# Rotary embedding of split heads: the first run of 1024 rows loaded and stored as two and six rows per partition

## The chip, the cores and the metric

One core of a Trainium2 chip runs the kernel. The metric is device time in microseconds (us) of one execution; the kernel before has a median of 161.52 us over three runs (161.49 to 161.65). The engines of the core work at the same time, each on its own list of instructions: PE (TensorE, matrix products), DVE (VectorE), ACT (ScalarE), POOL (GpSimd) and SP (SyncE, here only stores). They meet through semaphores. Data move between the large memory (HBM) and the on-chip memory of 128 partitions by 16 DMA engines, fed by two queues here: the loads that ACT issues and the stores that SP issues.

## The reference

The input `x` has 16 batches of 512 positions with 1024 values (16 heads of 64), `cos` and `sin` have one row of 32 values for each position. Each head is rotated:

```
x1, x2 = x[..., :32], x[..., 32:]          # in each head
out = concat(x1*cos - x2*sin, x1*sin + x2*cos)
```

All is float32: 33.6 MB are read and 33.6 MB written.

## The kernel before

**Rows, runs, tiles.** Two batches make a run of 1024 positions. A partition holds 8 neighbouring positions of it, so that a run is 8 "rows" of 128 partitions by 1024 values, and the whole is 8 runs or 64 rows, counted by `u`. The list `tiles` (lines 41 to 46) says in which pieces a run is loaded and stored: (run, first row, number of rows). Runs 1 to 6 go in one piece of 8 rows (4 MB, in each partition one stretch of 32 KB); runs 0 and 7 in two pieces of 4 rows (2 MB, 16 KB stretches). There are 10 loads and 10 stores. `x_sb` is a ring of 40 rows, in which a row is computed in place: five runs fit.

**What a row costs in instructions.** DVE multiplies the row by the cosines into PSUM (line 286, `mul`). POOL multiplies the row with its halves swapped by the signed sines into `t2_sb` (line 252), for two neighbouring rows in one instruction where `joined` says so; rows 0 to 3 and the last two are single. Row 3 of a run that is one piece is done by DVE instead (line 279; `V2`, `V_ROW`). The sum of the two products is made by DVE (line 297, `comb`) or, for rows with `PE2` (rows 1, 3 and 5 of a run, from row 4 on and up to row 59), by PE, which adds the second product through an identity matrix (line 216), and ACT, which moves the result back into `x_sb` (line 183). DVE's order is `mul(u)`, then `comb(u - 1)`. Before the first row of a tile (`r == 0`) both POOL and DVE wait for that tile's load, on `sem_in[t]`.

**The start.** ACT issues load 0, then the two loads of the tables `cos` and `sin`, then the other loads that fit the ring (lines 165 to 173). It makes `pick` from an identity matrix (line 176); PE waits for `pick` and both tables and spreads the tables over the partitions (line 200); ACT copies the sines to `s_sb` (lines 178 and 179). Only then can POOL and DVE start.

**Loads later on, and stores.** The loads of runs 5 to 7 need places of the ring that runs 0 to 2 give up. ACT issues them between its own instructions, after rows 17, 25 and 33, and waits first for all stores of run 0, 1 or 2 (lines 184 to 187; `stores_of` counts the stores of a run). SP goes through the rows, and at the last row of each tile it waits until all sums up to that row are made (`wait_added`) and issues the tile's store (lines 154 to 160).

Of the kernel before, what the change touches and what calls it, by code (L numbers as in the profile page):

```python
# [6 lines left out]
def bass_split_heads_rope_kernel(  # L7
# [21 lines left out]
    R1 = seq // P  # L29
    R2 = 2 * R1  # L30
# [10 lines left out]
    tiles = []  # L41
    for c in range(runs):
        if c in (0, runs - 1):
            tiles += [(c, 0, R1), (c, R1, R1)]
        else:
            tiles.append((c, 0, R2))
    NT = len(tiles)
# [300 lines left out]
```

## Time and profile before

| | us |
|---|---|
| median of three runs | 161.52 (161.49 to 161.65) |
| the profiled execution | 161.35 |
| its span, first to last instruction | 159.9 |
| POOL busy, of this line 252 | 131.8, 131.1 |
| DVE busy, of this lines 286, 297, 279 | 129.3, 76.7, 52.3, 7.3 |
| PE busy, ACT busy | 66.7, 23.7 |
| moved | 67.25 MB, 420 GB/s over the span |

The profile is one execution taken by the hardware profiler. Its page gives busy time for each engine and the span in 40 slices of 4 us, with the busy tenths of each engine and of the DMA engines. A share of the DMA engines a little over 1 comes from transfers that overlap on one engine. Other views of the same trace give instructions in order of time, the chain of work that ended last, busy time in chosen windows, and for a line that issues transfers the time from issue to landing. "Landing" is when the semaphore of a transfer has its full count.

### The profile page before, as it was taken

What the parts mean: (1) busy time and instruction counts of PE and PEld (TensorE: products, weight loads), DVE (VectorE), ACT (ScalarE), POOL (GpSimd) and SP (SyncE); (2) the same over time, 40 slices, a digit from 0 to 9 for tenths busy, and PEclk for the clock granted to TensorE, in tenths of its full rate; (3) what the DMA queues carried; (4) which work ended last, traced back from release to release, by engine and by line L of the source; (5) the groups of instructions that cost most, each with busy time, mean ns of one, the idle gap of its engine ahead of it and who ended that gap; (6) DMA issues with size and microseconds to landing.
All of it is one profiled execution on the core that took longest, in us unless ns stands there. A gap on an engine that the chain in (4) does not pass through costs nothing.

```text
span 159.9 us, 494 instructions
## 1 busy us (share of the span) xinstructions
PE 66.7 (42%) x94; PEld 22.6 (14%) x94; DVE 129.3 (81%) x115; ACT 23.7 (15%) x25; POOL 131.8 (82%) x41
## 2 busy tenths in 40 slices
PE   6050006338932762286209540098509860880000
PEld 1020002012301220122002110022102220220000
DVE  0009986799999999999799927999999989989700
ACT  0410000202220222020400204002500250031000
POOL 1009999999999999999999999599999999598000
PEclk9999999999995799569965998555985589567555
DMA  5999998999999999999999999999999999999896
GB/s 164 411 441 459 393 508 344 447 406 426 471 406 447 479 393 395 492 418 402 418 492 393 418 492 402 402 475 389 479 397 418 451 418 488 410 402 484 373 438 279
DMA packets 3169, 67.25 MB, mean 420 GB/s; under 512 B 352, under 2 KB 608, under 8 KB 608
## 3 DMA queue, kind: packets, MB, share of 16 engines
q10 hardware_dynamic: 1728, 33.69, 49.8%
q1 hardware_dynamic: 1440, 33.56, 48.7%
q14 instruction: 1, 0.01, 0.0%
HBM read 33.69 MB, written 33.55 MB: 420 GB/s over the span
## 4 chain that ended last, share of the span: by engine, by line
DMA 49%; DVE 16%; POOL 13%; issue 7%; PE 6%; ACT 2%; ACTq 1%; DVEq 0%; SPq 0%
DMA x_sb<-in_x_dram 27%; DMA out_dram<-x_sb 18%; POOL t_sb L252 13%; DVE x_sb L297 8%; DVE t_ps L286 6%; PE t_ps L216 5%; DMA stage<-in_sin_dram 4%; DVE t_sb L279 2%; ACT x_sb L183 1%; PE tab_ps L200 1%; ACTq L152 0%; ACTq L173 0%; ACT s_sb L178 0%; ACT s_sb L179 0%; DVE tab_ps L265 0%
## 5 line engine op out<-in xcount | busy, mean ns | idle before, releaser
L252 POOL TENSOR_TENSOR t_sb<-x_sb,s_sb 128x2048 f32<-128x2048 f32 (+1 forms) x35 | 131.1, 3775 | 14.9 <-ACT s_sb L179 10.3
L216 PE MATMUL t_ps<-t_sb,ident 128*128 128x512 f32 x84 | 61.9, 888 | 70.6 <-DVE t_ps L286 48.8
L286 DVE TENSOR_TENSOR t_ps<-x_sb,tab_ps 128x1024 f32<-128x1024 f32 x64 | 76.7, 1221 | 17.4 <-ACT s_sb L179 10.5
L297 DVE TENSOR_TENSOR x_sb<-t_ps,t_sb 128x1024 f32<-128x1024 f32 x43 | 52.3, 1219 | 3.2 <-POOL t_sb L252 3.1
L183 ACT ACTIVATE x_sb<-t_ps 128x1024 f32<-128x1024 f32 x21 | 21.3, 1024 | 111.6 <-PE t_ps L216 100.2
L216 PEld LDWEIGHTS t_ps<-t_sb,ident 128*128 128x128 f32 x84 | 20.7, 273 | 111.4 <-DVE t_ps L286 78.8
L279 DVE TENSOR_TENSOR t_sb<-x_sb,tab_ps 128x1024 f32<-128x1024 f32 x6 | 7.3, 1215 | 0.0
L200 PE MATMUL tab_ps<-stage,pick 128*128 128x256 f32 x4 | 2.0, 667 | 4.8 <-DMA stage<-in_sin_dram 4.8
L193 PE MATMUL t_ps<-zero 128*128 128x512 bf16 x6 | 2.7, 630 | 1.3 <-DVE zero L260 1.3
L200 PEld LDWEIGHTS tab_ps<-stage,pick 128*128 128x128 f32 x4 | 1.2, 324 | 5.9 <-issue 5.7
L176 ACT ACT_TABLE_LOAD x1 | 1.3, 1283 | 4.8 <-issue 4.8
L193 PEld LDWEIGHTS t_ps<-zero 128*128 128x128 bf16 x6 | 0.7, 138 | 2.3 <-DVE zero L260 1.2
L178 ACT ACTIVATE s_sb<-tab_ps 128x256 f32<-128x256 f32 x1 | 0.4, 384 | 4.4 <-PE tab_ps L200 4.4
L260 DVE MEMSET zero<- 128x256 uint32 x1 | 0.3, 272 | 0.9 <-PEq L330 0.9
L227 POOL MEMSET ident<- 128x128 f32 x1 | 0.2, 205 | 0.3 <-POOLq L330 0.3
L176 ACT ACTIVATE pick<-ident 128x256 f32<-128x256 f32 x1 | 0.4, 430 | 0.0
L179 ACT ACTIVATE s_sb<-tab_ps 128x256 f32<-128x256 f32 x1 | 0.4, 378 | 0.0
L229 POOL TENSOR_SCALAR_AFFINE_SELECT ident<-ident 128x128 f32<-128x128 f32 x1 | 0.3, 294 | 0.1
L330 POOL MEMSET const-float32-0.0<- 128x1 f32 x1 | 0.1, 99 | 0.3 <-issue 0.3
L265 DVE TENSOR_SCALAR tab_ps<-tab_ps 128x32 f32<-128x32 f32 x1 | 0.2, 189 | 0.0
L330 POOL MEMSET const-bfloat16-1.0<- 128x1 bf16 x1 | 0.1, 102 | 0.0
L330 POOL MEMSET const-uint8-127<- 128x1 uint8 x1 | 0.1, 102 | 0.0
(1 smaller groups left out, 0.1 us busy)
## 6 DMA issues: line engine op xcount, KB each, us to landing
x_sb<-in_x_dram ACTq DMA_DIRECT2D x6, 4096.0 KB, 33.5
out_dram<-x_sb SPq DMA_DIRECT2D x6, 4096.0 KB, 25.0
x_sb<-in_x_dram ACTq DMA_DIRECT2D x4, 2048.0 KB, 19.9
out_dram<-x_sb SPq DMA_DIRECT2D x4, 2048.0 KB, 14.9
stage<-in_cos_dram ACTq DMA_DIRECT2D x1, 64.0 KB, 7.3
stage<-in_sin_dram ACTq DMA_DIRECT2D x1, 64.0 KB, 7.0
```

The lines of the kernel that those rows point to most:

```text
L176: ae.activation(pick[:], ident[:].rearrange("q (s h) -> q h s", h=2)[:, :, None, :].broadcast_to([P, 2, 2, P // 2]), COPY).then_inc(sem_g, 1)
L178: ae.activation(s_sb[:, :, 0, :].rearrange("p (h r) d -> p h r d", h=2), tab_ps[:, :, 1], COPY, scale=-1.0)
L179: ae.activation(s_sb[:, :, 1, :].rearrange("p (h r) d -> p h r d", h=2), tab_ps[:, :, 1], COPY).then_inc(sem_s, 1)
L183: ae.activation(xs[:, u % RING, :], t1_ps[:, u % NT1, :], COPY).then_inc(sem_a, 1)
L193: pe.matmul(t1_ps[:, k, b * BANK:(b + 1) * BANK], zero[:, 0:P], zero[:], start=True, stop=True).then_inc(sem_w, 1)
L200: pe.matmul(tab_ps[:, h].rearrange("p c r d -> p (c r d)"), pick[:, h].rearrange("q b s -> q (b s)"), stage[:].rearrange("q c f -> q (c f) ...
L216: ins = pe.matmul(t1_ps[:, u % NT1, b * BANK:(b + 1) * BANK], ident[:], t2[:, b * BANK:(b + 1) * BANK], start=False, stop=True, skip_group ...
L252: pl.tensor_tensor(t2_sb[:, u % NT2:u % NT2 + n], x_sb[:, k:k + n, :, ::-1, :], table[:, :, None, :, :].broadcast_to([P, n, H, 2, HALF]), ...
L279: ve.tensor_tensor(t2_sb[:, u % NT2, :, :, :], swapped(k), over_heads(tab_ps[:, 0, 1, V_ROW - 1:V_ROW + 1, :]), mult)
L286: ve.tensor_tensor(t1_ps[:, u % NT1, :].rearrange("p (h d) -> p h d", d=HALF), x_sb[:, k, :, :, :].rearrange("p h t d -> p (h t) d"), tab_ ...
L297: ve.tensor_tensor(xs[:, k, :], t1_ps[:, u % NT1, :], t2_sb[:, u % NT2, :, :, :].rearrange("p h t d -> p (h t d)"), add,).then_inc(sem_v, 1)
L330: nc = _bacc.Bacc("TRN2", target_bir_lowering=False, num_devices=1)
```

## The change

Run 0 is cut after its second row in place of its fourth. Run 7 stays as it is.

```
     for c in range(runs):
         if c in (0, runs - 1):
-            tiles += [(c, 0, R1), (c, R1, R1)]
+            n = R1 // 2 if c == 0 else R1
+            tiles += [(c, 0, n), (c, n, R2 - n)]
         else:
             tiles.append((c, 0, R2))
```

Load 0 and store 0 become 1 MB (8 KB in a partition), load 1 and store 1 become 3 MB (24 KB). The waits for loads are then ahead of rows 0 and 2 in place of 0 and 4, and SP issues the first two stores after rows 1 and 7 in place of 3 and 7. `PE2` and `joined` go by row numbers and stay the same, as does `V2`, since neither piece of run 0 has eight rows. The number of instructions does not change.

More of the change, by code (lines that the diff above doesn't have):

```diff
@@ L43, in bass_split_heads_rope_kernel @@
         if c in (0, runs - 1):
-            tiles += [(c, 0, R1), (c, R1, R1)]
+            n = R1 // 2 if c == 0 else R1
+            tiles += [(c, 0, n), (c, n, R2 - n)]
         else:
```

## The prediction

> **What bounds the kernel now.** I read the page's slices first.
>
> ```profile
> span 159.9 us, 494 instructions
> ...
> PE 66.7 (42%) x94; PEld 22.6 (14%) x94; DVE 129.3 (81%) x115; ACT 23.7 (15%) x25; POOL 131.8 (82%) x41
> ...
> DMA  5999998999999999999999999999999999999896
> GB/s 164 411 441 459 393 508 344 447 406 426 471 406 447 479 393 395 492 418 402 418 492 393 418 492 402 402 475 389 479 397 418 451 418 488 410 402 484 373 438 279
> ```
>
> POOL and DVE look like bounds at some 82%, but the DMA engines are full in every slice except the first and the last ones. The busy time by windows says it sharper (us of the window; then each engine's busy time; last: clock, DMA share, GB/s):
>
> ```profile
> 0.00:2.00 2.00, 0.75 (x2) 0.28 (x3) 0.27 (x1) 0.00 (x0) 0.70 (x6) 1.00 0.39 74
> 2.00:4.00 2.00, 2.00 (x5) 0.46 (x3) 0.00 (x0) 0.00 (x0) 0.00 (x0) 1.00 0.78 254
> ...
> 30.00:40.00 10.00, 4.49 (x5) 1.67 (x6) 10.00 (x10) 1.39 (x2) 10.00 (x3) 1.00 1.01 428
> ...
> 120.00:130.00 10.00, 8.93 (x11) 3.24 (x12) 9.59 (x10) 2.05 (x2) 9.92 (x3) 0.54 0.98 419
> ```
>
> The reader is to see shares of 0.98 to 1.01 from 30 to 130 us: transfers that are ready wait for engines, whatever computes. Third, the chain of waits, for the two places where computing and transfers touch, the start and the end:
>
> ```profile
> 1.68 7.03 DMA stage<-in_sin_dram
> 8.71 0.14 issue
> 8.85 2.06 PE tab_ps L200 x4
> ...
> 11.67 9.48 POOL t_sb L252 x5
> ...
> 95.53 42.55 DMA x_sb<-in_x_dram
> 138.09 0.07 issue
> 138.16 6.85 POOL t_sb L252 x2
> ...
> 148.41 2.35 DVE x_sb L297 x2
> ```
>
> Computing starts at 11.67 because the sine table lands at 8.71, behind load 0 in ACT's queue (load 0: issued 0.80, 7.5 to landing, 8.3). It ends with the last load, landed at 138.09: the last store is issued at 150.83. Fourth, the landings of single transfers (a store's line, its time to landing):
>
> ```profile
> L160 SPq DMA_DIRECT2D out_dram<-x_sb x1: 376/376/376, 22.3 to 22.3; - x1
> ...
> DMA to landing us min/median/max: 19.3/19.3/19.3
> ...
> L160 SPq DMA_DIRECT2D out_dram<-x_sb x1: 332/332/332, 150.8 to 150.8; - x1
> ...
> DMA to landing us min/median/max: 9.1/9.1/9.1
> ```
>
> Store 0 lands at 41.6; by the same rows store 1 (issued 33.67, 22.6) at 56.3, the next at 75.6 and 95.1, the last three at 150.2, 155.1 and 159.9. Loads: 8.3, 13.56, 23.3, 36.9, 51.4, 70.4, 89.6, 109.0, 123.6, 138.1.
>
> **What a partition's run costs.** 128 partitions over 16 DMA engines are 8 runs on each. Load 2 (32 KB runs) takes 23.3 - 13.56 = 9.74, so 1.218 us a run; load 1 (16 KB) 13.56 - 8.71 = 4.85, 0.606 a run. Store 1 against loads of 32 KB takes 56.3 - 41.6 = 14.7 = 8 x (0.606 + 1.218 = 1.824) = 14.6; the 4 MB stores 19.3 to 19.5 = 8 x 2.436. So the two queues take turns run by run, whatever the size of a run. All runs together: 64 x 0.606 + 96 x 1.218 = 155.7, the tables 0.4 (8.71 - 8.3), and 8.3 - 4.85 = 3.45 before load 0 is at full rate: 159.5, against a span of 159.9. Only some 0.4 us is not pure transfer.
>
> The change makes runs of 8 and 24 KB, which the trace does not show. In proportion they cost 0.303 and 0.912; a run of 32 KB costs twice one of 16 KB, so no fixed part is seen. The upper bound is a whole table run (512 B, 16 of them in 0.41, 0.026) added to each of 16 runs, 0.4 us in all; the lower bound is that the shortfall of the second window (254 of 430 GB/s for 2 us, 0.8 us) halves with the smaller first runs, -0.4. I take 0, since the 16 and 32 KB rows are the nearest.
>
> **The change, part by part.** Instructions, waits and the order on each queue stay the same: ten loads, ten stores. Only two loads and two stores change size, and store 0 is due after row 1 in place of row 3.
>
> Start. Load 0 loses 8 x 0.303 = 2.43 us; the tables would land at 6.28. PE also needs ACT's `pick`, done at 6.52 (6.09 + 0.43, behind the table load at 4.79). So PE starts at 6.6 in place of 8.85: **2.25 us earlier**, POOL at 9.4. Bounds: 0 to 2.3. The page "DMA: Bandwidth & Descriptors" of the Trainium skill, section "Measured", gives 6.15 us for 1 MB and asks for pieces of at least 1 MiB; by its fit in "Anatomy of one DMA" (2.0 us fixed and bytes by 436 GB/s) an estimate for 1 MiB is 4.4 us. By the fit the tables would land at 5.6 and `pick` would still decide; by the line for 1 MB at 7.4 (0.8 + 6.15 + 0.4), and 1.3 us would be left of 2.25.
>
> Rows 2 and 3 now wait for load 1, whose bytes end where they did, at 13.56. POOL wants row 2 at 9.4 + 2 x 2.31 = 14.04, and is not held. DVE wants it at 15.26 - 2.25 = 13.01, is held 0.6, and makes it good in its idle 2.11 before 25.51. Behind its wait stand the rest of its own instructions, and row 1's addition: store 0 goes out at 16.0 (22.30 before). Store 1 goes out at 33.67 - 2.25 = 31.4.
>
> The store queue. Store 0 landed 19.3 after its issue, 14.7 of that in transfer: 4.6 us pass before an idle store queue gets its turns beside 32 KB loads. Now: store 0 from 20.6, 8 x (0.303 + 1.218) = 12.2, to 32.8; store 1 from 31.4 + 4.6 = 36.0, 8 x (0.912 + 1.218) = 17.0, to 53.0. Before it was 56.3. The next store (49.99 - 2.25 = 47.7, + 4.6 = 52.3) is there in time. So the **stores run 3.3 us ahead** from here on, and as the engines are full, every run that a store takes earlier a load takes later: the loads land 3.3 us later. Bounds: 1.0 if computing starts no earlier (55.3), and 4.0 where the next store's own start, 52.3, decides (a store 1 that follows store 0 with no gap).
>
> The middle. Loads 3.3 later: row 40's at 92.9. POOL wanted it at 93.0 (row 8 at 29.84, and four times three pairs of 4.49 and a single of 2.31), now at 90.8. DVE has by then gained more than 2.25, since its 4.14 us behind ACT's wait for the store of run 2 (95.1, now 91.8) moves with that store. POOL so waits about as long as computing is ahead (2.1 of 2.25), and row 48's load, at 112.3, is in the same relation: no net price here.
>
> The end. The last load lands at 138.1 + 3.3 = 141.4. Behind it: POOL's pair 4.51, then six DVE instructions (five starts 1.13 apart and 1.22: 6.9) and the issue, 0.15: the last store goes out at 153.0 in place of 150.83. Is that late? The store before it lands at 155.1 whatever happens, and 4.8 later the last one is through. An idle queue takes 7.5 for these 2 MB (load 0, a cold start); 4.85 of transfer and 1.4 to 1.9 of latency, an estimate from 4.6 less two 32 KB runs, make 6.5. So the end is 153.0 + 6.5 to 7.5 = 159.5 to 160.5, or the engines' own 159.9 where that is later: **+0 to +0.6**, and I take +0.2. The cover is the backlog in SP's queue, worth 9.1 - 6.5 to 7.5 = 1.6 to 2.6 us; the issue comes 2.2 later.
>
> Sum: start -2.25, hidden by full engines; loads +3.3, hidden by the backlog but for 0.2; span 160.1. The profiled execution took 161.35 us, 1.45 around the span, and the median is 161.52, 0.17 more: 160.1 + 1.45 + 0.15 = **161.7 us**.
>
> **Rivals.** A measurement of this kernel can tell some 0.2% (0.32 us) from no change.
>
> (a) Slower: the last store finds idle engines. One mechanism, stores ahead and loads behind; it decides once the loads are over 3.3 us late. At the upper bound of 4.0 and 7.5 for the store: 138.1 + 4.0 + 11.6 + 7.5 = 161.2, +1.3: **162.8 us**. If the store queue has no gap at all and the next store follows at 49.8, 6.5 late: 163.7 and 165.3 us. For it: the cover is thin by my own count, 1.6 to 2.6 against 2.2. Against: the engines are full, so a later load leaves no byte undone, only the last 2 MB badly placed. Chance 0.40.
>
> (b) Faster by the start: 2.25 reach the end, 161.52 - 2.25 = **159.3 us**. For: POOL has hardly a gap from 11.67 to 99.7. Against: the shares near 1.0, and the floor of 159.5 for the span. The page "Perfetto Trace Analysis" of the Trainium skill, "DMA Optimizations", says smaller pieces may help if the DMA engines are generally idle; here they are not, so by that rule nothing is gained either. Chance 0.04.
>
> (c) Faster within the floor: the 0.4 us over 159.5 go, and 0.4 of the start's shortfall: **160.7 us**. For: sixteen engines need not end as unevenly as now. Against: nothing in the change evens them. Chance 0.10.
>
> (d) The start does not move (tables or `pick` late): store 1 at 55.3, loads 1.0 later, inside the cover: **161.5 us**, counted with no change.
>
> **How the numbers follow.** Forecast with (d): 0.46; (a) 0.40; (b) and (c) 0.14. So faster 0.14, same 0.46, slower 0.40. The likeliest one's own range is 161.2 to 161.9. The range for all takes in (c) and most of (a): 160.8 to 163.6.
>
> **What would show it.** POOL's first product at 9.4; store 0 issued at 16.0 and store 1 at 31.4; store 1 landed near 53; the last load landed near 141.4; the last store issued near 153.0 and landed 6.5 to 7.5 later. Wrong would be: the last load no later than before (the turns are not by run), DMA shares below 0.95 in the middle (engines run dry), or a gap over 2 us in the DMA ahead of the last store.

## The result and the profile after

The changed kernel takes 1.0049 times the time before (95% interval 1.003 to 1.0069), +0.8 us with +0.5 to +1.1. The ratio rests on the executions near the kernel's fastest, two of seven at 162.16 and 162.25, since the others, from 164.75 to 168.55, are left out of it as disturbed (here and in all ratios below: those more than 1.5% above the fastest of the same kernel). The median of all seven is 165.23, beside 161.48 for before (161.16 to 161.65). The profile on record is of an execution of 165.29. First its page:

```profile
span 163.9 us, 493 instructions
...
DMA  5999999999999999999999999999999999999574
GB/s 178 392 444 418 450 382 416 424 446 442 430 436 414 480 418 400 464 408 456 432 400 464 424 440 432 416 456 400 424 452 432 412 432 408 480 424 408 256 324 204
```

The engines stay full through the middle, as before; the third and second slices from the end, 256 and 324 GB/s, are new (373 and 438 before). The busy time by windows shows that place (us; busy time of PE, PEld, DVE, ACT, POOL; clock, DMA share, GB/s), first before, then after:

```profile
152.00:154.00 2.00, 0.00 (x0) 0.00 (x0) 0.00 (x0) 0.00 (x0) 0.00 (x0) 0.50 1.07 459
154.00:156.00 2.00, 0.00 (x0) 0.00 (x0) 0.00 (x0) 0.00 (x0) 0.00 (x0) 0.50 0.99 426
156.00:158.00 2.00, 0.00 (x0) 0.00 (x0) 0.00 (x0) 0.00 (x0) 0.00 (x0) 0.50 0.97 418
```

```profile
152.00:154.00 2.00, 0.00 (x0) 0.00 (x0) 2.00 (x3) 0.00 (x0) 1.62 (x1) 0.50 0.97 418
154.00:156.00 2.00, 0.00 (x0) 0.00 (x0) 1.99 (x2) 0.00 (x0) 0.00 (x0) 0.50 0.12 49
156.00:158.00 2.00, 0.00 (x0) 0.00 (x0) 0.00 (x0) 0.00 (x0) 0.00 (x0) 0.50 0.63 270
158.00:160.00 2.00, 0.00 (x0) 0.00 (x0) 0.00 (x0) 0.00 (x0) 0.00 (x0) 0.50 0.99 418
```

From 154 to 156 the share is 0.12, so nearly all DMA engines have nothing to do, while DVE still works at the last rows: the last store is issued at 156.07 (150.83 before). A share in these windows counts each transfer record whole in the window in which it begins. That is why it can pass 1; it isn't that transfers overlap on one engine, where records overlap by some 4 ns only. Counted by overlap with the window, 154 to 156 has 0.21 after and 1.01 before. Why the last store is so late stands in the chain of waits:

```profile
133.42 4.52 POOL t_sb L253
137.94 6.50 another core or an unknown queue
144.44 0.07 issue
144.51 4.51 POOL t_sb L253
...
154.78 1.21 DVE x_sb L298
```

The 6.50 us are POOL's wait for the last load (the view does not name it, but its landing ends the wait): it landed at 144.44, 6.35 later than before.

A transfer's semaphore gets sixteen increments, one from each DMA engine, and the trace has the time of each. For the store before the last they are, in us, sorted:

```
before           154.1 154.1 154.2 154.2 154.3 154.3 154.3 154.3 154.3 154.3 154.4 154.4 154.5 154.6 154.9 155.1
after            154.3 154.3 154.3 154.3 154.4 154.4 154.4 154.5 154.6 154.7 154.8 154.9 155.1 155.2 155.5 159.0
```

Fourteen or fifteen engines are about as far as before; one is 4.5 us behind their middle. One was late with the last load too (middle 141.2, last 144.4), which delayed the last rows, and one with the last store (163.85, when the others were done by 162.4).

The increments carry no engine's name. But nearly every transfer record in the trace begins within 8 ns of the end of another one, so that the records can be strung, end to start, into sixteen chains, one for each engine. One chain ends its part of the last load at 142.87 (the other fifteen from 139.4 to 140.6), and the same chain ends its part of the last store at 163.50 (the others by 162.0). So one and the same engine is late.

Of the 6.35 us by which the last load is later, 4.0 are common to the engines (their middle: 141.2, before 137.3), and 2.4 come from the slowest, 3.2 behind the middle where it was 0.8.

### The profile page after: what moved, and what is told of

Its sections match the earlier page's. It is cut to its first block, busy times and chain, and to the rows that moved or that the text cites. A ratio compares the mean times of both kernels' runs of the same rounds, so it can differ in the third digit from the quotient of the medians.

```text
span 163.9 us, 493 instructions
## 1 busy us (share of the span) xinstructions
PE 66.3 (40%) x94; PEld 22.4 (14%) x94; DVE 129.4 (79%) x115; ACT 23.8 (15%) x25; POOL 131.7 (80%) x41
## 4 chain that ended last, share of the span: by engine, by line
DMA 47%; DVE 15%; POOL 14%; issue 7%; PE 6%; another core or an unknown queue 4%; ACT 1%; ACTq 1%; DVEq 0%; SPq 0%
DMA x_sb<-in_x_dram 29%; DMA out_dram<-x_sb 17%; POOL t_sb L253 14%; DVE t_ps L287 8%; DVE x_sb L298 6%; PE t_ps L217 6%; DVE t_sb L280 1%; ACT x_sb L184 1%; ACTq L174 1%; ACTq L153 0%; DVE tab_ps L266 0%; DVEq L297 0%; DVEq L284 0%; DVEq L146 0%
## 5 line engine op out<-in xcount | busy, mean ns | idle before, releaser
L217 PE MATMUL t_ps<-t_sb,ident 128*128 128x512 f32 x84 | 62.4, 893 | 71.4 <-DVE t_ps L287 55.2
L201 PE MATMUL tab_ps<-stage,pick 128*128 128x256 f32 x4 | 1.1, 405 | 2.4 <-ACT pick L177 2.4
L201 PEld LDWEIGHTS tab_ps<-stage,pick 128*128 128x128 f32 x4 | 0.7, 189 | 3.3 <-ACT pick L177 3.3
```

Source lines behind the costliest of these rows:

```text
L201: pe.matmul(tab_ps[:, h].rearrange("p c r d -> p (c r d)"), pick[:, h].rearrange("q b s -> q (b s)"), stage[:].rearrange("q c f -> q (c f) ...
L217: ins = pe.matmul(t1_ps[:, u % NT1, b * BANK:(b + 1) * BANK], ident[:], t2[:, b * BANK:(b + 1) * BANK], start=False, stop=True, skip_group ...
```

## The experiments

Two theories went into them. **A, the order:** the stores run ahead, the loads fall as much behind, and the last store finds idle engines. **B, one engine behind:** one of the sixteen falls behind the others. The "lead" of a kernel is how much earlier than before the last store of run 0 lands. Every ratio of this section is against executions of the kernel before on the same chip (held by one row, the two controls and run 0 stored in one piece ran on another chip than the other experiments); these stayed within 161.1 and 162.1 in all 46 of them.

**The changed kernel again.** No edit.

> The changed kernel once more. Theory A (order: the stores run some 3.3 us ahead, the loads land as much later, the last store finds idle DMA engines): last load landed near 141 to 142, all executions within 0.5 us of 162.2. Theory B (one DMA engine falls behind the other fifteen, and the last load and the last store wait for it): the last load lands 2 to 3 us after fifteen of its sixteen engines are done, and the executions spread over several us, 162 to 168, as in the profile on record (last load 144.4, 165.29 us).

1.0073 (1.0035 to 1.0112); ten executions from 161.59 to 169.86, median 164.51. The spread belongs to the kernel, and the granted clock does not go with it: 0.70 in the fastest, 0.73 in the slowest. A, with all of them within 0.5 us of 162.2, fails; B's spread is there. This profile is of an execution of 161.85, near the fastest, so it can be set against the prediction: the chain's start, two stores' lines with their times to landing (store 1, the last store), and the windows at the end:

```profile
2.16 11.77 DMA x_sb<-in_x_dram
13.94 0.07 issue
14.01 5.76 POOL t_sb L253 x3
```

```profile
L161 SPq DMA_DIRECT2D out_dram<-x_sb x1: 338/338/338, 31.4 to 31.4; - x1
DMA to landing us min/median/max: 20.6/20.6/20.6
...
L161 SPq DMA_DIRECT2D out_dram<-x_sb x1: 333/333/333, 153.8 to 153.8; - x1
DMA to landing us min/median/max: 6.6/6.6/6.6
```

```profile
152.00:154.00 2.00, 0.00 (x0) 0.00 (x0) 1.76 (x2) 0.00 (x0) 0.00 (x0) 0.50 0.96 410
154.00:156.00 2.00, 0.00 (x0) 0.00 (x0) 0.00 (x0) 0.00 (x0) 0.00 (x0) 0.50 0.90 377
```

Store 1 lands at 52.0 in place of 56.3, and the last store, 3.0 later than before, lands after 6.6 in place of 9.1: its cover is used up, and a share of 0.90 says that the engines were idle for a short while (counted by overlap 0.77, so 0.45 us for each engine). Here no engine is far behind (1.0 at the store before the last, 0.8 in before).

**Other cuts of run 0**, one line each: `n = R1 // 4` for one and seven rows, `n = R1 - 1` for three and five.

> Run 0 in pieces of one and seven rows. Row 1 then waits for load 1 (landed 14.4), so POOL's row 4 comes at 14.46 + 3 x 2.31 = 21.4, half a microsecond later than before; store 1 issued near 34.1, first transfer 4.0 later, 8 x (1.064 + 1.218) = 18.3 of transfer: done at 56.3, no lead over before. A: no later last load, time 161.5 (within 0.3 of before) and no spread. B (any uneven cut of run 0 lets an engine fall behind): 163 to 166 with a spread.

1.0134 (1.0101 to 1.0168), 162.85 to 165.01. A's 161.5 is missed by 1.9 us at the median (163.42), though the lead is gone (store 1 lands at 57.8) and the last load's middle engine is at 137.1, as before (137.3). The range is nearly that of B.

> Run 0 in pieces of three and five rows. Store 0 issued near 17.2, done 34.6; store 1 issued near 30.9, no gap between the two; the third store can start at 51.2, 4.8 us ahead of before (3.4 in the changed kernel). A: last load 4.8 later than before, 1.4 later than in the changed kernel, time 163 to 163.7, slower than the changed kernel. B alone: no order between the two, spread over several us.

1.0034 (1.001 to 1.0059) for the executions near the fastest, but the twelve fall into two groups: six from 161.23 to 162.86, six from 168.86 to 170.26. In the profiled execution, 161.34, the lead is the largest (store 1 at 51.5) and the last store is issued at 153.07, yet no engine is more than 0.5 behind, and the time is that of before. A's 163 to 163.7 is not there, nor its order between the kernels.

**Loads as changed, stores as before, and the reverse.** SP goes through a list of its own:

```
+    stores = [(0, 0, R1), (0, R1, R1)] + tiles[2:]
...
+            for c, r0, n in stores:
+                wait_added(sp, c * R2 + r0 + n - 1)
+                k = (c * R2 + r0) % RING
+                sp.dma_start(... outr[c][:, r0:r0 + n, :] ..., ... x_sb[:, k:k + n] ...)
```

> Loads of two and six rows as changed, stores of four and four rows as before. Store 0 issued near 20.4, stores done at 54.2, a lead of 1.8 us. A: last load 1.8 later than before, hidden by the backlog of stores: 161.5 to 161.8, no spread. B as far as it comes from the uneven loads: 163 to 166 with a spread.

164.16 to 169.04, median 167.7: the slowest of all, with a lead of only 0.9 (store 1 at 55.4). The chain and the windows of its end, for an execution of 167.3:

```profile
135.48 4.52 POOL t_sb L255
140.00 6.46 another core or an unknown queue
146.46 0.07 issue
```

```profile
154.00:156.00 2.00, 0.00 (x0) 0.00 (x0) 2.00 (x3) 0.00 (x0) 1.64 (x1) 0.50 0.35 147
156.00:158.00 2.00, 0.00 (x0) 0.00 (x0) 2.00 (x2) 0.00 (x0) 0.00 (x0) 0.50 0.08 33
```

The same picture, larger: the last load's middle engine is done at 139.3, its last one at 146.5, and the engines wait idle at a share of 0.08. The engine behind is 5.9 late at the store before the last.

The reverse keeps `tiles` of before and has `stores = [(0, 0, R1 // 2), (0, R1 // 2, R2 - R1 // 2)] + tiles[2:]`.

> Loads of four and four rows as before, stores of two and six rows as changed; the start stays at 11.7. Store 0 issued near 17.7, store 1 near 33.7 and done near 55.3, a lead of 1.0 us. If uneven loads let a DMA engine fall behind: 161.2 to 161.9 in every execution. If uneven stores do it: 162 to 168 with a spread. If the lead of the stores is all that counts: 161.5.

1.0127 (1.01 to 1.0154), 162.56 to 164.05. The second expectation is the nearest: even loads are no shield, and uneven stores are enough to cost 2 us, though with a small spread. One engine is 2.7 behind in the profile (the second slowest: 0.8), and the engines are not idle ahead of the last store: here the late engine alone makes the loss.

**An early start without an uneven piece.** The two table loads go ahead of load 0:

```
+            for i, (table, sem) in enumerate(((cos, sem_cos), (sin, sem_sin))):
+                ae.dma_start(stage[:, i, :], ...).then_inc(sem, 16)
             for t, (c, r0, n) in enumerate(tiles):
...
-                if t == 0:
-                    for i, (table, sem) in enumerate(...):
-                        ae.dma_start(stage[:, i, :], ...).then_inc(sem, 16)
```

> The kernel before, pieces of four and four, with the two table loads issued ahead of load 0: the first products wait only for load 0 and start near 9.0 in place of 11.7, so stores run about 2.7 us ahead without any uneven piece. If the uneven cut is the cause of the spread: no spread, and by the lead alone (last load near 140.8, hidden but for some tenths) 161.4 to 162. If the early start of the stores is the cause: spread 162 to 168 as in the changed kernel.

1.0048 (1.003 to 1.0066), 161.84 to 162.7: near A's 161.4 to 162 for an early start, and without the large spread. Store 1 lands at 53.6, the last load's middle engine at 140.5 (137.3 before). But the loss is not A's. The windows of its start and end, for the execution of 162.7:

```profile
0.00:2.00 2.00, 0.75 (x2) 0.28 (x3) 0.27 (x1) 0.00 (x0) 0.70 (x6) 1.00 0.05 15
2.00:4.00 2.00, 1.99 (x5) 0.45 (x3) 0.00 (x0) 0.00 (x0) 0.00 (x0) 1.00 0.82 182
...
154.00:156.00 2.00, 0.00 (x0) 0.00 (x0) 0.00 (x0) 0.00 (x0) 0.00 (x0) 0.50 1.07 459
```

The last store, issued at 153.47, finds busy engines. What is missing is moved at the start: 15 and 182 GB/s in these 4 us, 74 and 254 before, together 0.26 MB or 0.6 us at 430 GB/s. The rest of this execution's 1.35 us is an uneven end: the slowest engine is 1.4 behind (0.8 before). The 0.6 us is also about the loss of the usual execution (median 161.96, before 161.32). So A's number came near for another reason.

**Stores held back.** In the changed kernel SP's list is `list(tiles)`, and the two stores of run 0 wait for two rows more: `wait_added(sp, c * R2 + r0 + n - 1 + (2 if c == 0 else 0))`.

> The changed kernel with the two stores of run 0 held back by two rows: store 1 issued near 37.5, first transfer 41.5, done near 58.5, so the stores run 2.5 us behind before in place of ahead, and the loads land 2.5 earlier. If the lead is the cause: 161.0 to 161.6, no spread. If the uneven loads are the cause: 163 to 168 with a spread, the last load's slowest engine late whatever the lead.

1.0036 (1.0019 to 1.0053), ten executions from 161.54 to 162.5. The loads come 2.1 earlier than before (middle engine 135.1), the last store at 152.82 finds busy engines, and the large spread is gone. Uneven pieces alone therefore do not make it. The 161.0 to 161.6 expected for the lead are reached by three of the ten. The windows at the end:

```profile
152.00:154.00 2.00, 0.00 (x0) 0.00 (x0) 0.74 (x1) 0.00 (x0) 0.00 (x0) 0.50 0.99 426
154.00:156.00 2.00, 0.00 (x0) 0.00 (x0) 0.00 (x0) 0.00 (x0) 0.00 (x0) 0.50 1.04 442
```

Held by one row (`1 if c == 0`):

> The changed kernel with the two stores of run 0 held back by one row: store 1 issued near 34.0, done near 55.0, a lead of 1.3 us between that of the changed kernel (3.5 to 4.2) and that of two rows held (-2.6). If the lead sets the time: 161.5 to 161.9 and little spread, between those two. If it is a matter of which engine meets which, not of the lead: a spread over more than 2 us.

1.013 (1.0108 to 1.0152), five executions from 163.44 to 164.12 and one of 169.23. By the ratio, a lead of 1.7 is worse than both the changed kernel's 3.4 to 4.3 and the -2.5 of two rows held. By the median, 163.7, it lies between the two (164.5 and 161.8), so this run alone does not decide against the lead. Across all variants the lead does not order the times: tables first has 2.7 and a median of 162.0, loads of two and six with stores of four and four 0.9 and 167.7.

The two controls hold back the stores of the kernel before, and of the one with the tables first:

> Control: the kernel before (four and four, start at 11.7) with the two stores of run 0 held back by two rows, done near 63.7, 7.4 behind before. The DMA engines are full either way and the last load lands earlier: 161.2 to 161.7, no spread. If holding itself costs, as the 161.55 of the fastest executions with held stores against 161.1 of before could say: 161.6 to 162.

1.0084 (1.0062 to 1.0106), 162.36 to 163.37: slower, and above both expectations.

> Even pieces, tables loaded first (start near 8.7), and the two stores of run 0 held back by two rows: done near 60.8, 4.5 behind before. If the lead of the stores cost tables_first its +0.5%: 161.2 to 161.6. If the early start costs it in another way: 161.9 as without holding.

1.0086 (1.0063 to 1.0109), 162.64 to 163.37, again above both. Holding back costs here, and the waits of this kernel show how (us in total, times, the longest), with a window of its end:

```profile
ACT x_sb L184 <- DMA out_dram<-x_sb: 16.4, 2, 9.2
...
DVE t_ps L287 <- ACT x_sb L184: 13.5, 6, 6.1
```

```profile
154.00:156.00 2.00, 0.00 (x0) 0.00 (x0) 1.15 (x2) 0.00 (x0) 0.00 (x0) 0.50 0.62 262
```

ACT waits 16.4 us (11.4 before) for stores whose place in the ring the later loads need, DVE then waits for ACT's results, and the last store goes out at 155.2 though the last load landed early (134.6). All engines end within 0.2 us of each other, so no engine is behind. The span of 161.6, 1.6 more than before, has its cause in engines without work: 0.7 us more than before at the start, as in tables first, some 0.6 about 142 and some 0.6 ahead of the last store, of which the more even end gives a part back. The last of the three is A's end, reached from the other side.

**Run 0 stored in one piece**, `stores = [(0, 0, R2)] + tiles[2:]`, loads as changed:

> Loads of two and six rows as changed, run 0 stored in one piece of eight rows: issued near 31.8, done near 55.3, a lead of 1.0 us, and all store runs of the first five runs are 32 KB. If the lead is the cause: 161.4 to 161.9, no spread. If the uneven loads make an engine fall behind whatever the stores: 163 to 168 with a spread.

1.0057 (1.0035 to 1.0079), 162.25 to 163.18: uneven loads without the large spread, but above the 161.4 to 161.9 of the lead. Store 0 landed at 57.0, so there was no lead either.

**The last run in six and two rows** (`n = R1 // 2 if c == 0 else R2 - R1 // 2`), which covers a late last load:

> The changed kernel with the last run in pieces of six and two rows: behind the last load stand only two rows (some 7 us in place of 11.6), and the last store is 1 MB, so that a late last load is hidden. If the fast executions' +0.7 comes from the last store finding idle DMA engines: the fastest executions fall to 161.3. If an engine that falls behind makes the rest: its own bytes end late all the same, and the spread up to 166 and more stays.

1.0059 (1.0042 to 1.0076), 161.97 to 162.4 four times, then 164.92 and 167.03. The end is covered, as SP's line and the window show:

```profile
150.81 0.33 SPq L161 DMA_DIRECT2D out_dram<-x_sb  x1
```

```profile
154.00:156.00 2.00, 0.00 (x0) 0.00 (x0) 0.00 (x0) 0.00 (x0) 0.00 (x0) 0.50 1.14 492
```

The last store is issued when it was before, the engines are full up to 158, and yet the fastest execution is at 161.97, not at the expected 161.3. A late last store is therefore not all of the cost. The spread stays, as the second expectation had it. In this execution's trace the 0.6 us of span over before are several small terms: 0.3 of longer transfers (the mean over the engines), 0.1 at the start, 0.2 of a less even end.

The fourteen profiled executions side by side (us; "store 1": the last store of run 0; "behind": the last of the sixteen engines after their middle, at the store before the last):

| kernel | profiled execution | store 1 landed | last load, middle / last engine | last store issued | behind |
|---|---|---|---|---|---|
| before | 161.35 | 56.3 | 137.3 / 138.1 | 150.83 | 0.8 |
| changed, again | 161.85 | 52.0 | 141.2 / 142.2 | 153.84 | 1.0 |
| changed, on record | 165.29 | 52.9 | 141.2 / 144.4 | 156.07 | 4.5 |
| one and seven | 162.85 | 57.8 | 137.1 / 139.4 | 152.75 | 1.3 |
| three and five | 161.34 | 51.5 | 140.1 / 141.4 | 153.07 | 0.5 |
| loads 2+6, stores 4+4 | 167.30 | 55.4 | 139.3 / 146.5 | 158.08 | 5.9 |
| loads 4+4, stores 2+6 | 163.34 | 53.7 | 138.6 / 141.3 | 152.90 | 2.7 |
| tables first | 162.70 | 53.6 | 140.5 / 141.9 | 153.47 | 1.4 |
| held by two rows | 161.56 | 58.8 | 135.1 / 135.9 | 152.82 | 0.6 |
| held by one row | 163.50 | 54.6 | 139.2 / 141.5 | 153.10 | 2.2 |
| before, held | 162.96 | 62.6 | 135.5 / 137.3 | 154.52 | 1.5 |
| tables first, held | 162.97 | 62.4 | 133.8 / 134.6 | 155.23 | 0.1 |
| loads 2+6, one store | 162.33 | 57.0 | 137.7 / 140.2 | 151.85 | 1.2 |
| last run six and two | 161.97 | 53.1 | 140.4 / 142.3 | 150.81 | 0.9 |

The last two columns account for most of the time. Where the last store is issued by 153.1, the execution's time less "behind" lies from 160.6 (before) to 161.6 (one and seven); it is highest, 162.9, where the last store is late with no engine behind (tables first, held). The lead, from the third column, moves the middle engine of the last load in A's direction in all rows but one (loads 2+6, one store), though not one for one (before, held: a lead of -6.3 moves it by -1.8), and the times do not follow it.

"One engine" fits the profile on record and the two mixed kernels (loads 2+6 with stores 4+4, and the reverse). It is too narrow elsewhere: held by one row, six of the sixteen are about 1 us or more behind the middle, and with one and seven rows three are.

## Why the prediction came out as it did

The start: 2.25 earlier was forecast, POOL's first product is at 9.25 in the repeated run (11.67 before), 2.4 earlier (8.3 in the profile on record, where PE's four products for the tables took 405 ns each and not 667). PE waited for `pick`, as forecast. Load 0 landed 4.9 us after its issue; of the two other times that the prediction names for it, 4.4 was the nearer and 6.15 did not come.

Rows 2 and 3: load 1 landed at 13.9 and not 13.56; POOL was held by 0.1 and not at all, DVE by 1.0 and not 0.6. It cost nothing further on.

The store queue: store 0 issued at 16.3 (16.0), store 1 at 31.4 (31.4) and landed at 52.0 (53.0). The turns run by run and the gap of some 4 us before the first transfer gave this to a microsecond. The lead, forecast as 3.3 with 4.0 as its upper bound, was 4.3.

The loads: the last one at 142.2 where 141.4 was forecast, so 4.1 later than before and not 3.3. POOL waits 11.1 us for three loads (3.0 at row 40, 3.6 at row 48, 4.6 at row 60; before 1.9, at row 60). The forecast was 2.1 at row 40 and the same relation, at no net price, at row 48. POOL was 2.3 ahead of before up to row 32, as forecast, then 0.7 behind it at row 40 and 2.0 at row 48: the waits took more than had been gained.

The end: last store at 153.8 (153.0), 6.6 to its landing (6.5 to 7.5), span 160.4 (160.1). Part of this is luck: the lower figure, 6.5, rests on a latency of 1.4 to 1.9 "from 4.6 less two 32 KB runs", but 4.6 - 2 x 1.218 is 2.2, which gives 7.0. The issue came 0.8 later than forecast, and the shorter landing hid part of it.

So the forecast of 161.7 was near the repeated execution's 161.85, and 0.5 below the 162.2 of the two executions behind the first ratio. By that ratio the loss of 0.8 us (0.5 to 1.1) is above the 0.32 us that the prediction counts as no change, and 162.2 lies between its likeliest outcome (161.2 to 161.9) and rival (a) (162.8). The usual execution it did not foresee: five of the seven, and six of the ten of the repeated run, lie above the 163.6 at which its widest range ends. One of its own signs of being wrong, a gap of over 2 us ahead of the last store, is there in the profile on record: most engines fall idle between 153.9 and 154.8 and stay so until 156.9.

The step that failed, for these executions, is the cover: "The cover is the backlog in SP's queue, worth 9.1 - 6.5 to 7.5 = 1.6 to 2.6 us; the issue comes 2.2 later." It treats sixteen engines as one, with one time at which their backlog ends, and a load as landed when an average engine is done. Measured, each load lands with its slowest engine, and the end of the kernel is that of the slowest engine, which was 0.8 behind the middle before and 1.0 and 4.5 in two executions of the changed kernel. The mechanism of rival (a), a last load too late and a last store on idle engines, is shown by the share of 0.12. Its condition, loads more than 3.3 us late, was met in both executions by the middle engine alone (4.0), and cost little in the one (161.85); what made the other 165.29 was the engine 3.2 us behind at the last load, which (a) does not have. The small loss is at least in part the same end with engines closer together: in the execution of 161.85, 0.5 over before, they are idle for 0.45 us ahead of the last store. Terms of 0.1 to 0.3 at the start, in longer transfers and in a more even finish stand beside it, and as the run with the last pieces of six and two rows shows, a loss of this size can stay when that end is covered.

The forecast that nothing of the early start reaches the end held in every run: no variant with an earlier start beat the kernel before, nor did any other version. What stays open is why one engine, or a few, fall behind in some orders and executions and not in others. Uneven loads alone, uneven stores alone and the lead alone were each tried, and none of them orders the results.

## What to carry to other kernels

Where the DMA engines are full from end to end, an earlier start only changes the order of the transfers; ask which transfer is then served later, and whether the last rows wait for it. Look at the sixteen engines one by one: a transfer is there when the slowest is done, and a kernel whose last store has 2 us of cover has none if one engine is 3 us behind. Several executions of a change belong to its price, since a rearrangement that is harmless in the best of them can cost 8 us in others.

## What was not expected of the hardware

In the profile on record, 32 KB runs of stores, 1.213 us elsewhere, took 1.33 to 1.67 us in three stretches (61 to 72, 91 to 107 and 115 to 140 us), at most one such run for each turn of a pair of queues; with the few others before 141 us they add 5.2 us. In the sixteen chains of records (see the result), sixteen of the seventeen long runs from 91 us on lie in one chain, the one that ends last. Its runs between 30 and 150 us, loads and stores, take 3.5 us more than at the usual rate; for the middle chain that is 0.1. The runs from 61 to 72 us cannot be given to it for certain, since two chains come within 5 ns of each other there. With loads of four and four and stores of two and six rows it is the same: 2.9 us in one chain, 0.3 in the middle one. So the engine is behind because its own transfers take longer; why they do is open. From 141 us on, when only stores are left, no run of 32 KB is longer by more than 0.05. Before, two such stores come to 0.35 and 0.23 us.
